# Projection blocks of the forgetting-attention heads taken in pairs, seven pairs with 2x2 block products; weight sums formed by transfers in memory

## Chip, core and metric

One core of one Trainium2 chip runs one layer of a hybrid decoder trunk. The metric is the device time of one execution in microseconds. The engines are PE (TensorE, its weight loads shown apart as PEld), DVE (VectorE), ACT (ScalarE), POOL (GpSimd) and SP (SyncE, which here only issues transfers).

## What is computed

A layer of width 2048 over 16 meta tokens and 512 tokens. A normalised input goes through one input projection, whose columns feed three kinds of heads: six gated DeltaNet heads, five gated linear attention heads (GLA) and five forgetting-attention heads. Each head's output is multiplied by a SiLU gate, and all go through one output projection, a residual add and a final norm.

```python
def hybrid_layer(x, norm_w, w_in, ...):
    h = rms_norm(x, norm_w)
    h = jnp.pad(h, ((0, 0), (PAD, 0), (0, 0)))
    proj = (h @ w_in).astype(f32)
    (dq, dk, dv, dz, db, da, gq, gk, gv, gz, gl, fq, fk, fv, fz, ff) = split_cols(proj)
    ...
    o_dn = gated_head_norm(o_dn, dz, dn_norm_w.astype(f32))
    ...
    o_gla = gated_head_norm(o_gla, gz, gla_norm_w.astype(f32))
    ...
    o_fox = forgetting_attention(to_heads(fq, FOX_HEADS) * FOX_D ** -0.5, to_heads(fk, FOX_HEADS),
                                 to_heads(fv, FOX_HEADS), log_f)
    o_fox = o_fox.reshape(fz.shape) * jax.nn.silu(fz)
    o = jnp.concatenate([o_dn, o_gla, o_fox], axis=-1)[:, PAD:].astype(x.dtype)
    return x + o @ w_out
```

Everything is float32, to float32 accuracy.

## The kernel before

**Numbers.** A float32 operand of a large product is split into two parts of a shorter type: `hi`, a rounded copy written by ACT, and `lo`, the rest, written by DVE (`split`, lines 148 to 151). A product is then three: hi x hi, hi x lo, lo x hi.

**Input projection.** The transposed input lies on chip for the whole projection as 16 row blocks of 128 features (`xh[k]`, `xl[k]`, each 128 x 528: 16 meta tokens and 512 tokens). The weights are in blocks of 128 output columns, each in two halves of 8 row blocks (`w_in[b, half]`, 128 x 1024, 512 KB). `load_half` (line 140) issues a half's load on SP's queue into `raw`, and splits it into `hi` and `lo`; each of these three has two buffers. `inproj` (221) runs a block. With the meta tokens it makes two results of 264 columns, so 16 x 3 x 2 = 96 products; without them (`meta=False`: fq, fz, gates) one result of 512 columns with 48 products. Results go to banks of the pool `psb`, which has four; `evac` (320) multiplies them by the row factor `rstd` of the norm on their way out.

**Order.** The blocks run in the order of `_cols`: for each of two groups of three DeltaNet heads dz, then dk (`dn_keys`), dv (`dn_values`), dq (`dn_queries`); then gz, the GLA blocks by pairs of heads (`gla_pair`), then for each forgetting head fk, fv, fq, fz (`fox_head`). The small work of a stage (scores, state products, transposes) runs between the products of later blocks. A planner orders all instructions of each engine when the kernel is built, by program order as priority and by its own estimates of time. On the chip each engine takes its instructions in that fixed order. `behind` and `place` tie some small products behind a numbered product of the projection; in particular `behind(mm, PM[g])` ties the first product `pm` of a group's triangular inverse behind the 308th (group 0) or 319th (group 1) product after `dn_queries`.

**The triangular inverse** (`dn_inverse`, line 535). Blocks of the matrix `an` go through memory (`scr`) into `ab`, DVE inverts them by 60 dependent steps (lines 556 and 558), the result goes through memory (`sc2`) into `iv`, and the products `pm`, `pl`, `pn`, `pu` put the pieces together. These transfers are on ACT's queue.

**SiLU** (`silu`, line 330) begins with a maximum on POOL (line 334), has three steps on ACT and one product on DVE.

**Output projection.** Heads 0 to 7 of the list dz, gz, fz (the six DeltaNet gates and two GLA gates; `SH = 8`) go through it as 2x2 blocks by seven products (`product`, 1151); the other eight as plain products (`run`, 1094). The seven products need sums of weight blocks, `tw`. `weight_sums` (426) forms them in the stage of forgetting heads 0 to 3: it loads 256 KB parts into `ws`, subtracts on DVE (432) and stores them to `tw`. `first_sums` (452) forms the sums of the heads on DVE in forgetting head 4. The gated heads stay on chip in the pool `zp` until then.

## Time and profile before

| | |
|---|---|
| three runs | 1011.84, 1010.10, 1010.04 us; median 1010.1 |
| profiled execution | 1010.53 us |
| its span, first to last instruction | 1008.8 us |
| granted TensorE clock, mean | 0.998 |
| bytes moved by transfers | 128.13 MB, 127 GB/s over the span |
| input projection, forgetting-attention stage | 631 to 828 us |
| GLA stage | 486 to 631 us |
| output projection | 828 to 1001 us |

The profiler gives each instruction's start and duration. A group of rows shows line, engine, operation, out<-in by the program's names, shape, count, then busy time in us, the mean duration of one in ns, the idle time of the engine just before these, and what ended that idle time. Products overlap: the spacing of their starts is what a product costs in a stream, not its duration. Of transfers the rows give count, size of one in KB and the median time from issue to landing in us.

### The profile page before, as it was taken

The page shows a single profiled execution, that of the slowest core. Times are in us where ns is not written, and L with a number is a line of the kernel's source. Part 1 is how long each engine was busy: PE and PEld are TensorE (multiplying, and loading weights), DVE is VectorE, ACT ScalarE, POOL GpSimd, SP SyncE. Part 2 cuts the span into 40 slices and gives each one's busy share as a digit, 9 for nine tenths or more (in the row PEclk, how much of TensorE's full clock was granted, in tenths as well). Part 3 has the DMA queues.
Part 4 walks back from the last instruction along what each step waited for, and adds up shares of the span by engine and source line. Part 5 has one row for each costly group of instructions (what it writes and reads, how often), then busy time and mean ns, then how long its engine had stood idle before and what let it go on. Part 6 is the DMA issues. An engine that isn't in the chain of part 4 may idle for free.

```text
span 1008.8 us, 19003 instructions
## 1 busy us (share of the span) xinstructions
PE 995.7 (99%) x7614; PEld 898.7 (89%) x7614; DVE 618.2 (61%) x1342; ACT 433.1 (43%) x948; POOL 138.6 (14%) x141
## 2 busy tenths in 40 slices
PE   9999999999999999999999999999999999999996
PEld 7899999899999888898989988889898988888885
DVE  6366767865566985244646474655363747677673
ACT  7654533434456334244445444342323244354354
POOL 0021411211112322101111010100101010000060
PEclk9999999999999999999999999999999999999999
DMA  9623233233222223231221272543362635466634
GB/s 351 229 67 119 82 93 96 102 101 104 75 86 75 94 90 101 68 94 59 84 64 50 66 244 82 189 138 93 120 226 95 237 119 188 127 193 226 181 109 167
DMA packets 53357, 128.13 MB, mean 127 GB/s; under 512 B 11949, under 2 KB 15197, under 8 KB 53268
## 3 DMA queue, kind: packets, MB, share of 16 engines
q1 hardware_dynamic: 39008, 115.30, 34.5%
q10 hardware_dynamic: 14260, 11.61, 4.1%
q8 instruction: 60, 0.98, 0.4%
q14 instruction: 29, 0.24, 0.1%
HBM read 113.32 MB, written 13.44 MB: 126 GB/s over the span
## 4 chain that ended last, share of the span: by engine, by line
PE 92%; DVE 3%; ACT 1%; DMA 1%; POOL 1%; issue 1%; ACTq 1%; SPq 0%; DVEq 0%; POOLq 0%
PE pp L207 57%; PE pa L1068 5%; PE pq L1068 4%; PE pp L261 4%; PE pt L1068 4%; PE ps L1068 2%; PE pss L822 1%; PE pr L1068 1%; POOL stgz L334 1%; PE pgate L361 1%; PE pfo L990 1%; PE pfa L957 1%; DVE wlo L151 1%; DVE ot L556 1%; PE pg L523 1%
## 5 line engine op out<-in xcount | busy, mean ns | idle before, releaser
L207 PE MATMUL pp<-xl,whi 128*128 128x264 f32 (+2 forms) x1456 | 378.1, 310 | 0.0
L207 PE MATMUL pp<-xh,whi 128*128 128x264 f32 (+2 forms) x1456 | 376.3, 310 | 0.8 <-DVE fqk L325 0.7
L207 PE MATMUL pp<-xh,wlo 128*128 128x264 f32 (+2 forms) x1456 | 375.4, 309 | 0.4 <-DVE wlo L151 0.4
L207 PEld LDWEIGHTS pp<-xh,whi 128*128 128x128 f32 x1456 | 243.1, 188 | 15.1 <-issue 1.4
L207 PEld LDWEIGHTS pp<-xl,whi 128*128 128x128 f32 x1456 | 244.3, 189 | 13.6 <-issue 0.2
L207 PEld LDWEIGHTS pp<-xh,wlo 128*128 128x128 f32 x1456 | 243.7, 188 | 14.1 <-DVE wlo L151 0.8
L150 ACT CAST whi<-raw 128x1024 fp32r<-128x1024 f32 x110 | 115.3, 1048 | 184.7 <-PE pp L207 158.1
L151 DVE TENSOR_TENSOR wlo<-raw,whi 128x1024 fp32r<-128x1024 f32 x110 | 134.4, 1222 | 88.8 <-ACT whi L150 78.2
L334 POOL TENSOR_SCALAR stc<-cv 128x528 f32<-128x528 f32 (+1 forms) x18 | 28.2, 1566 | 138.2 <-DVE cv L418 115.2
L418 DVE SCALAR_TENSOR_TENSOR cv<-pb,cpk,cv 128x528 f32<-128x528 f32 (+1 forms) x54 | 40.7, 755 | 0.7
L1068 PE MATMUL pa<-whio,ol 128*128 128x512 f32 x72 | 28.5, 396 | 0.0
L1068 PE MATMUL pa<-wloo,oh 128*128 128x512 f32 x72 | 28.3, 393 | 0.0
L325 DVE TENSOR_TENSOR pb<-pp,rstd 128x264 f32<-128x264 f32 (+1 forms) x36 | 13.7, 423 | 23.3 <-PE pp L207 23.3
L432 DVE TENSOR_TENSOR ws<-ws 128x512 f32<-128x512 f32 x32 | 21.6, 686 | 9.7 <-DMA ws<-in_w_dn 9.6
L150 ACT CAST whis<-raws 128x1024 fp32r<-128x1024 f32 x16 | 16.8, 1051 | 24.8 <-PE pq L1068 9.7
L151 DVE TENSOR_TENSOR wlos<-raws,whis 128x1024 fp32r<-128x1024 f32 x16 | 19.5, 1222 | 12.7 <-ACT whis L150 12.7
L1068 PE MATMUL pa<-whio,oh 128*128 128x512 f32 x72 | 26.6, 399 | 0.0
L977 ACT CAST fphi<-pfx 128x384 fp32r<-128x384 f32 (+2 forms) x20 | 8.0, 399 | 41.0 <-PE pfx L974 38.2
L966 ACT ACTIVATE fp<-fp,fsm 128x144 f32<-128x144 f32 (+3 forms) x20 | 11.5, 574 | 29.8 <-DVE fsm L965 29.7
L150 ACT CAST whio<-rawo 128x1024 fp32r<-128x1024 f32 x13 | 13.7, 1051 | 24.1 <-PE pa L1068 12.8
L334 POOL TENSOR_SCALAR stfz<-zfz 128x512 f32<-128x512 f32 x5 | 10.6, 2126 | 94.9 <-ACT whi L150 47.8
L1092 POOL TENSOR_TENSOR acc<-acc,fw 128x512 f32<-128x512 f32 x3 | 4.6, 1564 | 135.2 <-ACT sqf L1089 135.2
(439 smaller groups left out, 1642.7 us busy)
## 6 DMA issues: line engine op xcount, KB each, us to landing
raw<-in_w_in SPq DMA_DIRECT2D x110, 512.0 KB, 3.3
ws<-in_w_dn SPq DMA_DIRECT2D x32, 256.0 KB, 4.7
tw<-ws SPq DMA_DIRECT2D x32, 256.0 KB, 3.5
rawo<-in_w_out SPq DMA_DIRECT2D x13, 512.0 KB, 3.4
raws<-tw SPq DMA_DIRECT2D x12, 512.0 KB, 4.6
xt<-in_xtok SPq DMA_DIRECT2D x8, 512.0 KB, 8.7
rawa<-in_w_dn SPq DMA_DIRECT2D x8, 512.0 KB, 3.6
xs<-in_xT SPq DMA_DIRECT2D x7, 528.0 KB, 7.1
```

The source lines that it names most:

```text
L150: pace[0] = A.copy(hi, raw).ins
L151: pace[1] = V.tensor_tensor(out=lo, in0=raw, in1=hi.bitcast(F32), op=ALU.subtract).ins
L207: mm = PE.matmul(p_[:, :nt], wt[:, j * m : (j + 1) * m], xx[k][:, t0 : t0 + nt], start=(k == 0 and wt is hi and xx is xh), stop=(k == KT - ...
L261: mm = PE.matmul(ps[:, :S], wt[:, j * P : (j + 1) * P], xx[k][:, NM:T], start=(k == 0 and wt is hi and xx is xh), stop=(k == KT - 1 and wt ...
L325: V.tensor_tensor(out=o, in0=p_[rows], in1=rstd[rows, t0 : t0 + n], op=ALU.mult)
L334: G.tensor_scalar_max(t, src, LOW)
L361: PE.matmul(pgate[a][:, :HT], wg[k // 8][:, k % 8, :], xx[k][:, a * HT : (a + 1) * HT], start=(k == 0 and xx is xh), stop=(k == KT - 1 and ...
L418: V.scalar_tensor_tensor(out=c, in0=pb[:, t0 + w : w + T], scalar=cwc[:, blk, w : w + 1], in1=c, op0=ALU.mult, op1=ALU.add)
L432: sub = lambda o, a, b: V.tensor_tensor(out=o, in0=a, in1=b, op=ALU.subtract)
L523: PE.matmul(pg[:r, j * r : (j + 1) * r], kT[:, j, ts], kT[:, j, ts], start=True, stop=True)
L966: A.activation(pr[:, : m + P], pr[:, : m + P], AF.Exp, bias=sm[:, 2:3], accum_out=sm[:, 3:4])
L1068: PE.matmul(p_, o_[:, s], w_, start=(first and n == 0), stop=(last and n == 2), skip_group_check=True)
```

## The change

It has three parts.

**Pairs of projection blocks.** For forgetting heads 1 to 4 the blocks are taken as pairs (fk, fq) and (fv, fz). The first pair of head 1 runs as before (`SKIP = 1`), which leaves seven. `inproj_pair` treats a pair as a 2x2 block product: output blocks (one, two) by token halves of 264 columns, over row blocks k and k + 8. For 4 of the 8 pairs of row blocks (`NK = 4`) it uses seven products with sums of weights and of inputs; the other four pairs of row blocks are plain. Its weights come as six tiles, split in halves of 512 columns; some are negated in the split. The columns of the meta tokens of the second block are left out where they are not needed (`dead`). The results are scaled by `rstd` afterwards, on POOL and DVE.

```diff
+    def inproj_pair(n, c1, c2, tmp):
...
+            for c in range(0, o, 512):
+                cuts.append(slice(c, c + 512))
+                split(raw[:, cuts[-1]], hi[:, cuts[-1]], lo[:, cuts[-1]], neg)
+            return [(hi[:, c], lo[:, c]) for c in cuts]
+
+        def mm(p_, w, xx, first=False, last=False, cols=slice(0, HT)):
+
+            hi, lo = w
+            todo = [(hi, j, i) for j in range(len(xx)) for i in range(2)] + [(lo, j, 0) for j in range(len(xx))]
+            for i, (wt, j, part_) in enumerate(todo):
+                m = PE.matmul(p_[:, cols], wt[:, j * P : (j + 1) * P], xx[j][part_][:, cols],
+                              start=first and i == 0, stop=last and i == len(todo) - 1, skip_group_check=True)
+                order.append(m.ins)
...
+        dead = slice(NM, HT)
+        nm = f"{b1}_"
+        a, b = bank("a"), bank("b")
+        w1, w2 = tile_of("1", both(b1, head_))
+        mm(a, w1, xs_(up, lo_), True, True)
+        A.copy(ta, a[:, :HT])
+        mm(b, w2, xs_(dn, lo_), True)
+        def two():
+            nonlocal d
+            d = bank("d")
+            w1, w2 = tile_of("2", ti[n][:, 0:2], neg=True)
+            mm(d, w1, sums("t1"), True, True)
+            A.copy(tb, d[:, :HT])
+            mm(a, w2, sums("t2"), False, True)
+            V.tensor_tensor(out=tb, in0=a[:, :HT], in1=tb, op=ALU.add)
+
+        def three():
+            nonlocal c
+            c = bank("c")
+            w1, w2 = tile_of("3", both(b1, rest_))
+            mm(b, w1, xs_(r0, lo_))
+            mm(b, w2, xs_(r1, lo_), False, True)
+            V.tensor_tensor(out=c1[:, lo_], in0=b[:, :HT], in1=ta, op=ALU.add)
+            mm(c, w1, xs_(r0, hi_), True)
+            mm(c, w2, xs_(r1, hi_))
+
+        c = d = None
+        for f in (three, two) if n < LATE else (two, three):
+            f()
+        w1, w2 = tile_of("4", ti[n][:, 2:4])
+        mm(a, w1, xs_(up, hi_), False, True)
+        A.copy(ta, a[:, :HT])
+        mm(c, w2, xs_(dn, hi_), False, True)
+        V.tensor_tensor(out=c1[:, hi_], in0=c[:, :HT], in1=tb, op=ALU.add)
+        w1, w2 = tile_of("5", w_in[b2, 0][:, rest_], w_in[b2, 1][:, head_], neg=True)
+        mm(d, w1, xs_(r0, hi_))
+        mm(a, w2, sums("t4"), cols=dead)
+        mm(a, w1, xs_(r0, lo_), cols=dead)
+        w1, = tile_of("6", w_in[b2, 1][:, rest_], neg=True)
+        mm(d, w1, xs_(r1, hi_), False, True)
+        V.scalar_tensor_tensor(out=c2[:, hi_], in0=d[:, :HT], scalar=-1.0, in1=ta, op0=ALU.mult, op1=ALU.subtract)
+        mm(a, w1, xs_(r1, lo_), False, True, cols=dead)
+        A.activation(c2[:, dead], a[:, dead], AF.Copy, scale=-1.0)
```

In `fox_head` the seven pairs and their scaling:

```diff
+                inproj_pair(n, kT, qT, qk[:, 1])
+                G.tensor_tensor(out=kT, in0=kT, in1=rstd, op=ALU.mult)
+                V.scalar_tensor_tensor(out=qT[:, NM:], in0=qT[:, NM:], scalar=float(P) ** -0.5, in1=rstd[:, NM:],
+                                       op0=ALU.mult, op1=ALU.mult)
+            if h == H1:
+                x_last(True)
+            v = row(f"vf{h}")[:, :T]
+            zr = row(f"zfz{h}")[:, :T]
+            inproj_pair(n + 1, v, zr, qk[:, 1])
+            G.tensor_tensor(out=v, in0=v, in1=rstd, op=ALU.mult)
+            vhi, vlo, v3, vm = values(v)
+            G.tensor_tensor(out=zr[:, NM:], in0=zr[:, NM:], in1=rstd[:, NM:], op=ALU.mult)
```

**Input sums.** `x_sums(k)` forms three sums of input blocks for row block k with nine operations on POOL, and splits each (ACT and DVE). It stands before GLA pair 1 for k = 0, before pair 2 for k = 1 and 2, and in forgetting head 0 for k = 3. `x_last` replaces the second token half of `xh[0..3]` and `xl[0..3]` by a sum, formed in head 0 on DVE and written in head 1 before its pair. The sums of k = 0 to 2 take buffers of `zp` (12 instead of 11). To free those, the eight heads of the 2x2 output blocks are stored to memory (`zd`) when they are done, and loaded again after the last projection block.

**Weight sums in memory.** `weight_sums` goes. For the pairs (`ti`) and for the output projection (`tw`), sums are formed by a copy from memory to memory on SP's queue and transfers that add to their destination, on POOL's queue. Signs are chosen so that all are additions. Each `load_half` issues up to `rate` = 2 such steps, from `dn_values(0)` on, tied behind the split of that load in the planned order (`paced`, an order only, not a wait). A group of jobs goes stage by stage: all copies, then the additions that read only weights, then the two that read earlier results.

```diff
+    def steps_of(jobs):
+        for kind, out_, in_ in jobs:
+            if kind:
+                paced(G.dma_start(out=out_, in_=in_, accum_op=ALU.add, max_dma_last_dim=2048))
+            else:
+                paced(nc.sync.dma_start(out=out_, in_=in_))
+            yield 1
+
+    def in_jobs(n):
+        h, one, two = PAIRS[n]
+        w = lambda key, half: w_in[BLOCK_OF[key, h], half][:, :KC]
+        o = [ti[n][:, i] for i in range(4)]
+        return [[(0, o[0], w(two, 0)), (0, o[2], w(one, 0)), (0, o[1], w(one, 0)), (0, o[3], w(one, 1))],
+                [(1, o[0], w(two, 1)), (1, o[2], w(two, 0))], [(1, o[1], o[0])], [(1, o[3], o[1])]]
+
+    def out_jobs(j):
+        w = lambda i, J: w_dn[J, 2 * j + i]
+        o = [tw[j, i] for i in range(4)]
+        return [[(0, o[0], w(0, 1)), (0, o[2], w(1, 1)), (0, o[1], w(1, 1)), (0, o[3], w(1, 0))],
+                [(1, o[0], w(0, 0)), (1, o[2], w(0, 1))], [(1, o[1], o[0])], [(1, o[3], o[1])]]
...
+    AHEAD = {(0,0):(2,(-1,-2,-3,-4),(-5,-6,-7),(0,1,2,3))}
+    XSUM = {1: (0,), 2: (1,2), 9:(3,)}
```

`KC` is 512 columns, so a step of a pair moves 256 KB and one of the output projection 512 KB. The order is four pairs, three pairs, then the four output blocks.

With other signs, the output projection subtracts instead of adding where it takes up the second half of its columns (`take`), and `first_sums`, `differences` and `s4` follow. `first_sums` moves to POOL and to the third step of the output projection. In `fox_head` the buffer of the next head's keys and queries is taken early (`ahead_`), and in `gla_pair` the tile `a32` shares the buffer of `ot`.

241 lines of the change are left out of this document (177 added, 64 removed).

## The prediction

> **What bounds the kernel now.** I read the page's sums first, then the chain that ended last, then stage windows, then who waits for whom.
>
> ```profile
> span 1008.8 us, 19003 instructions
> PE 995.7 (99%) x7614; PEld 898.7 (89%) x7614; DVE 618.2 (61%) x1342; ACT 433.1 (43%) x948; POOL 138.6 (14%) x141
> PE 92%; DVE 3%; ACT 1%; DMA 1%; POOL 1%; issue 1%; ACTq 1%; SPq 0%; DVEq 0%; POOLq 0%
> ```
>
> TensorE is busy for 995.7 of 1008.8 us and is 92% of the chain. Busy alone doesn't prove that it streams, so I looked at starts. Two stretches of the projection, one of products 264 columns wide (a row merges two), one 512 wide, and three products 256 wide:
>
> ```profile
> 731.12 0.41 PE L207 MATMUL pp<-xh,whi 128*128 128x264 f32 x2
> ...
> 738.98 0.41 PE L207 MATMUL pp<-xh,wlo 128*128 128x264 f32 x2
> 700.42 0.39 PE L207 MATMUL pp<-xh,wlo 128*128 128x512 f32 x1
> ...
> 708.07 0.39 PE L207 MATMUL pp<-xh,wlo 128*128 128x512 f32 x1
> 715.15 0.28 PE L990 MATMUL pfo<-fphi,vhi 128*128 128x256 f32 x1
> 715.26 0.28 PE L990 MATMUL pfo<-fplo,vhi 128*128 128x256 f32 x1
> 715.38 0.29 PE L990 MATMUL pfo<-fphi,vlo 128*128 128x256 f32 x1
> ```
>
> The first stretch holds 64 products between its quoted starts (32 rows of two): 7.86 / 64 = 0.1228 us each. The second holds 33: 7.65 / 33 = 0.2318. The third shows 0.115. The slope between the first two is (0.2318 - 0.1228) / 248 = 0.00044 us a column, so a 248-wide product should take 0.1228 - 16 x 0.00044 = 0.1158. These are spacings; the 0.41 or 0.39 in a row is a duration that overlaps its neighbours.
>
> TensorE's waits on anything else are small:
>
> ```profile
> PE pp L207 <- DVE fqk L325: 0.7, 1, 0.7
> PE psn L694 <- ACT y L690: 0.6, 1, 0.6
> PE pp L207 <- DVE wlo L151: 0.4, 1, 0.4
> 631.00:828.00 197.00, 196.31 (x1232) 176.34 (x1232) 105.54 (x261) 65.46 (x128) 15.17 (x16) 1.00 0.46 154
> ```
>
> The window is the forgetting-attention stage, 631 to 828 us (columns: length, then busy time of PE, weight load, DVE, ACT, POOL, then granted clock, DMA share, GB/s). TensorE is full there at a granted clock of 1.00; DVE is at 54%, ACT at 33%, POOL at 8%. So what counts is TensorE work removed, less new waits of TensorE; work moved between the other engines counts only through such waits.
>
> **The products.** Before, a pair such as fk and fq costs 96 products of 264 and 48 of 512: 96 x 0.1228 + 48 x 0.2318 = 11.79 + 11.13 = 22.92 us. After, I count the calls of `mm` in `inproj_pair`: fifteen, each of 4 x 3 products, so 180. Three calls (36 products) write only columns 16 to 263, the others 264: 144 x 0.1228 + 36 x 0.1158 = 17.68 + 4.17 = 21.85. A pair saves 1.07 us, seven save 7.5. If the 248-wide ones took a full 0.1228, it would be 0.82 a pair, 5.7 in all; at the 0.115 of the 256-wide row, 1.10 and 7.7.
>
> The Trainium skill's page "TensorE: Matmul & The Clock Gate", section "Back-to-back issue gap", speaks against such a trade: for streams of weight load and product it gives some 81 ns at 128 columns and 131 at 512, so width would cost little and count much. As an estimate from that page, 264 columns would be about 99 ns; a pair would go from 15.8 to 17.8 us and the seven would lose 14. The rows disagree, with 0.1228 against 0.2318.
>
> **The weight tiles of a pair.** Six tiles feed a pair instead of four, in halves of 512 columns; four of them feed only 24 products, 24 x 0.1228 = 2.95 us, where before each fed 5.6 to 5.9.
>
> ```profile
> raw<-in_w_in SPq DMA_DIRECT2D x110, 512.0 KB, 3.3
> L150 ACT CAST whi<-raw 128x1024 fp32r<-128x1024 f32 x110 | 115.3, 1048 | 184.7 <-PE pp L207 158.1 <-issue 10.0 <-DVE vpm L633 8.7
> L151 DVE TENSOR_TENSOR wlo<-raw,whi 128x1024 fp32r<-128x1024 f32 x110 | 134.4, 1222 | 88.8 <-ACT whi L150 78.2 <-PE ps L653 4.3 <-ACT gsq L897 4.2
> SPq L142 <- DVE wlo L151: 524.2, 86, 13.2
> ws<-in_w_dn SPq DMA_DIRECT2D x32, 256.0 KB, 4.7
> ```
>
> Today SP waits for a free raw buffer and ACT for TensorE to give a buffer back (158.1 of 184.7 us idle), so supply has room. One buffer's round is 3.3 + 1.05 + 1.22 = 5.6 us, two buffers give a tile every 2.8: just under 2.95, well under the pair's mean of 21.85 / 6 = 3.6. With a load of 4.7 us (the slowest weight row) it is (4.7 + 2.27) / 2 = 3.5, late by 0.54 us at each of three short tiles in a row (6, 1, 2): 1.6 a pair, 11.3 in all. I take 0.1 a pair, 0.7, since the mean has room and half tiles let the first product start after 512 columns; bounds 0 and 11.3.
>
> **The banks.** A product that accumulates onto a bank must wait until the copy out of it is done. For six pairs 24 to 48 products stand between. Pair 0 runs block three ahead of two, so tile 4's products onto bank a stand right behind the DVE sum that reads a. That is the kind of wait in the row "PE pp L207 <- DVE fqk": 0.7 us, once. Bounds 0 and 0.7 for each pair, 4.9.
>
> **Work off TensorE.** ACT and DVE split 38.5 full tiles where they split 28 (seven pairs by 5.5 and 4): 10.5 x 1.22 = 12.8 us more on DVE, and four reads of a bank a pair. DVE loses the weight sums (32 x 0.686) and the work moved to POOL.
>
> ```profile
> L432 DVE TENSOR_TENSOR ws<-ws 128x512 f32<-128x512 f32 x32 | 21.6, 686 | 9.7 <-DMA ws<-in_w_dn 9.6
> L1092 POOL TENSOR_TENSOR accs<-accs,fw 128x512 f32<-128x512 f32 x9 | 13.3, 1511 | 0.0
> 486.00:631.00 145.00, 142.96 (x1894) 130.79 (x1893) 88.74 (x190) 65.89 (x173) 16.49 (x12) 1.00 0.31 99
> ```
>
> POOL's nine operations of 264 columns for each of four row blocks (`x_sums`), scaled from 1.511 us for 512, are 9 x 0.78 = 7 us a block. Three blocks fall into 486 to 631 us, where POOL is busy 16.5 of 145. POOL's scaling of kT and v (1.6 us each) and DVE's of qT are hidden by the next pair's 21.85 us or by the head's scores. I cost all this, `x_last`, the eight gates stored and read back, and `first_sums` on POOL (needed some 30 us later) at nothing. Without cover, a late kT costs its 1.6 us in each of four heads.
>
> **The traffic in memory.** 88 steps go out at two a weight load over 44 loads, from dv of the first group to the last gz. They move 28 copies of 256 KB and 16 of 512, and as many accumulations, and end some 240 us before the first pair needs them. Each is issued behind a split, copies on SP, accumulations on POOL. Behind a copy on SP stand the weight loads, which have room as shown. Behind an accumulation on POOL stand silu's first step and the masks; POOL idles 86% of the time, but one place has no room: the triangular inverse of group 1. The chain of waits:
>
> ```profile
> 341.27 1.79 DMA scr<-an
> 354.85 3.50 POOL stgz L334
> 366.48 2.65 POOL stgz L334
> 377.65 2.61 POOL stgz L334
> 386.61 5.46 DMA sc<-ab
> 395.14 0.58 DVE L568 STREAM_TRANSPOSE iv<-iv 128x384 f32<-128x384 f32 x1 [5.62 <-DMA iv<-sc]
> 396.57 0.95 PE L574 MATMUL pm<-iv,an 32*32 32x32 f32 x48
> 214.22 0.58 DVE L568 STREAM_TRANSPOSE iv<-iv 128x384 f32<-128x384 f32 x1 [3.14 <-DMA iv<-sc]
> 220.48 0.95 PE L574 MATMUL pm<-iv,an 32*32 32x32 f32 x48
> ```
>
> The inverse is a serial run on DVE, and three silus of gz stand in its queue, each held by POOL (stgz). Its result is ready at 395.72 and TensorE takes it at 396.57: 0.85 us of room, where group 0 has 220.48 - 214.80 = 5.7. TensorE takes its work in order, so what comes later than 0.85 us is paid in full. The last 16 accumulations, of 512 KB, go out over the eight loads of gz1 to gz4, right there.
>
> No row shows what an accumulation costs POOL. Nearest are ACT's own issues (0.33 us at L541, in the row below) and stgz itself at 2.61:
>
> ```profile
> 338.42 0.33 ACTq L541
> 338.78 1.93 ACTq L541
> ```
>
> Three silus, each behind one issue, give 1.0 to 7.8 us, and transfers scr, sc and iv (1.79, 5.46 and the end of sc at 392.07 to 395.14 = 3.07; sum 10.3) may stretch by nothing up to double. Less the 0.85: 0.1 to 17 us. I take 1.5: half the silus behind an issue of some 1.0 us (the mean of the two ACT issues is 1.1) and a tenth of the transfers, 1.5 + 1.0 - 0.85 = 1.6; it lies near the low end because POOL is idle before each stgz and the accumulations stop before sc goes out.
>
> The page "DMA: Bandwidth & Descriptors" of the Trainium skill, section "Anatomy of one DMA — SWDGE (gpsimd) path", gives a DMA from GpSimd some 2.0 us plus its bytes over 436 GB/s. By it a 512 KB accumulation is an estimated 3.2 us and 16 of them 51 us in a stretch of some 45; the transfers would be slowed to the end of the chain. No row of before can show it.
>
> **The sum**, against the profiled execution's 1010.53 us (span 1008.8, 1.7 around it; 0.4 above the median 1010.1 of 1010.04 to 1011.84): -7.5 products, +0.7 tiles, +0.7 bank, +1.6 inverse = -4.5. From the median: 1005.6.
>
> **Rivals.** (1) *No new wait*: the chain keeps inside its 0.85 us and the tiles are in time: 1010.1 - 7.5 = 1002.6. For it: POOL and DMA are mostly idle (a DMA share of 0.31 and 0.46 in the windows). Against: the chain's small room.
> (2) *Short tiles starve*: loads of 4.2 us make a tile cost 3.24 instead of 2.95, three a pair, 21 x 0.29 = 6.1 in place of 0.7: 1005.6 + 5.4 = 1011.0, no change. For it: the 2.8 us round; against: SP's long waits.
> (3) *The inverse is late, slower than before*: scr, sc and iv double under the copies and accumulations (+10.3), silus add 1.5: 11.8 - 0.85 = 11.0 in place of 1.6: 1015.0. It decides from a delay of 1.6 + 4.5 + 2 + 0.85 = 9.0 us on. For it: it all passes at 341 to 395 us; against: the traffic is spread over loads.
> (4) *Weight loads show*: 36 more per pair that nothing hides at 0.188 us (its row below) are 6.8 a pair, 47 in all: 1053. Loads start every 0.12 us today beside products, so hardly. The Trainium skill's rule on the gap, above, leads the same way.
> (5) *Sums not ready*: tile 2 waits for memory. The last accumulation is due before 400 us, the first pair runs near 690; 290 us of room leave it next to nothing.
>
> ```profile
> L207 PEld LDWEIGHTS pp<-xl,whi 128*128 128x128 f32 x1456 | 244.3, 189 | 13.6 <-issue 0.2
> ```
>
> **How the numbers follow.** Forecast 0.50, (1) 0.20, (2) 0.13, (3) 0.15, (4) and (5) together 0.02. About 0.2%, 2 us, is what a measurement tells from no change. Faster: 0.50 + 0.20 = 0.70; same 0.13; slower 0.17. The forecast's own range is 1003.6 (inverse and tiles free, bank paid) to 1008. For 8 in 10 I reach down to 1001.8 (rival 1 with 7.7 and ordering) and up to 1011.8 (all of rival 2); left out is most of (3).
>
> **What would show it.** Right: in a stretch of pairs 264-wide starts 0.123 apart and 248-wide 0.115 to 0.117; seven pairs' products 153 us in all against 160; a wait of TensorE near pm of group 1 of 1 to 2 us; bank waits below 1 us. Wrong: waits of TensorE on wlo or whi in the pairs above 2 us in sum (rival 2), a wait at pm above 5 us or stgz starting late behind POOL's issues (rival 3), or 264-wide starts further apart than 0.125.

## The result, and the profile after

| | before | after |
|---|---|---|
| median of six runs each, same chip | 1010.06 us (1009.27 to 1011.84) | 1014.4 us (1013.65 to 1016.73) |
| ratio | | 1.0046, 95% interval 1.0036 to 1.0057 |
| profiled execution | 1010.53 us | 1014.15 us |
| granted TensorE clock, mean | 0.998 | 0.995 |
| bytes moved | 128.13 MB | 152.57 MB |

The kernel became slower by 0.46%, where 0.45% faster was forecast; 1014.4 lies outside the range of 1001.8 to 1011.8. The sums on the page of the changed kernel, and its chain that ended last:

```profile
span 1012.4 us, 19797 instructions
PE 991.5 (98%) x7866; PEld 908.5 (90%) x7866; DVE 642.7 (63%) x1389; ACT 460.4 (45%) x1041; POOL 224.5 (22%) x236
PE 49%; DVE 2%; issue 1%; DMA 1%; ACT 1%; ACTq 0%; SPq 0%; DVEq 0%
```

TensorE is busy for 4.2 us less than before in a span that is 3.6 us longer. The chain's shares add up to little more than half, so it breaks off on the way back and can't be read as before. The view of TensorE's waits can (total, times, longest, in us):

```profile
PE pm L735 <- DVE iv L729: 2.7, 1, 2.7
PE py L849 <- DVE zz L845: 1.9, 1, 1.9
PE pp_b L533 <- DVE wlo L167: 1.1, 1, 1.1
PE pp_a L533 <- ACT fqk L575: 1.0, 1, 1.0
```

Two of these four were in the sum (pp_b is the wait for a tile, pp_a the wait for a bank, both in the first pair). The one at pm was there with a smaller size, and the one at py not at all.

**Where the time went.** For six groups of TensorE's products, the start of the last one, as the rows grouped by tile give it, in us (for "first pa", the start of the first of L1295's products with `wloo`). The two right-hand columns are experiments told below.

| | before | after | output sums left out (e6) | output sums first, begun earlier (e11) |
|---|---|---|---|---|
| pu, end of the inverse of group 1 | 421.6 | 425.6 | 422.1 | 423.9 |
| po, end of the DeltaNet stage | 480.7 | 488.0 | 481.7 | 483.5 |
| pgt, end of the GLA stage | 631.7 | 641.1 | 634.2 | 634.3 |
| first pa, start of the output projection | 828.8 | 830.2 | 823.4 | 823.4 |
| last pz | 1000.4 | 1004.1 | 995.6 | 995.6 |

Read as lags behind the kernel before: +4.0 at pu, +7.3 at po, +9.4 at pgt, +1.4 at the output projection, +3.7 at the end. So the stage with the pairs did gain 8.0 us, its own new waits included, but it began 9.4 us late; 7.3 of that arose in the DeltaNet stage, which the change was not about. The next two groups of windows, first of the kernel before, then of the changed one (length, busy time of PE, weight load, DVE, ACT, POOL, then granted clock, DMA share, GB/s), show that place:

```profile
396.00:410.00 14.00, 13.62 (x204) 11.16 (x203) 5.57 (x9) 6.48 (x11) 0.00 (x0) 1.00 0.21 76
410.00:486.00 76.00, 75.42 (x590) 70.97 (x589) 27.63 (x67) 29.55 (x97) 8.08 (x7) 1.00 0.24 74
```

```profile
396.00:410.00 14.00, 11.29 (x169) 9.68 (x169) 4.17 (x7) 6.84 (x11) 0.42 (x2) 0.88 0.61 184
410.00:486.00 76.00, 73.49 (x600) 69.11 (x588) 28.82 (x68) 27.78 (x87) 16.96 (x17) 0.98 0.55 147
401.42:404.83 3.41, 3.41 (x15) 3.19 (x14) 0.37 (x2) 2.37 (x4) 0.00 (x0) 0.50 0.86 298
466.27:469.68 3.41, 3.41 (x18) 3.41 (x18) 2.14 (x6) 0.00 (x0) 0.00 (x0) 0.50 0.70 127
```

TensorE stands still for 2.7 us of the first window. The DMA share is 0.61 and 0.55 where it was 0.21 and 0.24. And the granted clock, 1.00 throughout before, is at one half for 3.41 us twice: the drops begin 1.7 and 2.0 us after the two waits have ended, and each costs up to 3.41 x 0.5 = 1.7 us of products.

**The wait at pm.** The timeline of the changed kernel along the inverse of group 1 (start, duration, engine; in brackets the idle time before and what ended it):

```profile
386.46 0.26 ACTq L721 DMA_DIRECT2D sc<-ab  x1
...
394.66 0.38 ACTq L724 DMA_DIRECT2D iv<-sc  x1
...
398.47 0.69 DVE L354 TENSOR_TENSOR zsgz<-zgz,stgz 128x512 f32<-128x512 f32 x1 [9.05 <-ACT stgz L353]
399.08 0.57 DVE L729 STREAM_TRANSPOSE iv<-iv 128x384 f32<-128x384 f32 x1
399.70 0.95 PE L735 MATMUL pm<-iv,an 32*32 32x32 f32 x48 [2.71 <-DVE iv L729]
```

The store sc is issued at 386.46, before at 386.61: DVE's inverse and the silus in its queue were on time. From the issue of sc to that of iv it now takes 8.20 us (before 5.48), from there to the transpose 4.42 (before 3.05). Together that is 4.1 us more, against 0.85 us of room. The two parts have different causes.

The first 2.7 us are the store sc, and it is held up ahead of its first packet. The view of transfers of the changed kernel between 386.5 and 391.4 us shows packets of one queue alone, SP's (packets, MB, share of the 16 engines):

```profile
q1 hardware_dynamic: 176, 1.46, 85.0%
```

On that queue a weight load and two copies of 512 KB had been issued at 384.8, 385.2 and 385.7 us. By the packet records of the trace, the first packet of sc starts 4.97 us after its issue and the last ends 2.71 us after that; in the kernel before it is 1.27 and 3.85 us. So sc is not slower while it moves.

The other 1.4 us are not the transfer iv: its packets, with those of `xm` behind it, end 2.9 us after its issue, and before 3.0. They are the order of DVE's queue. Here `zsgz`, the last step of a silu, stands ahead of the transpose of iv, and it waits for ACT's silu steps, which stand behind the issues of iv and `xm` in ACT's queue. In the kernel before it stands behind the transpose of 395.14:

```profile
396.30 0.69 DVE L338 TENSOR_TENSOR zsgz<-zgz,stgz 128x512 f32<-128x512 f32 x1
```

The planner made this order when the kernel was built. Of the runs below, e3, e4 and e8, which have two output copies just ahead of sc as well, have it too, and all others have the order of before.

**The wait at py.** The timeline of the changed kernel, then that of the one before, for the fetch `eg`, the decay factors of a chunk of the DeltaNet recurrence:

```profile
448.16 2.75 POOL L436 DMA_DIRECT2D tw<-in_w_dn  x3
...
456.46 0.37 ACTq L834 DMA_DIRECT2D eg<-gd  x1
462.02 0.52 ACT L835 ACTIVATE eg<-eg 128x384 f32<-128x384 f32 x1 [4.69 <-DMA eg<-gd]
...
462.58 0.17 DVE L837 COPY egl<-eg 128x3 f32<-128x3 f32 x1 [6.40 <-ACT eg L835]
...
464.29 1.01 PE L849 MATMUL py<-zz,uf 128*128 128x128 f32 x6 [1.94 <-DVE zz L845]
```

```profile
452.52 0.37 ACTq L673 DMA_DIRECT2D eg<-gd  x1
456.08 0.53 ACT L674 ACTIVATE eg<-eg 128x384 f32<-128x384 f32 x1 [2.68 <-DMA eg<-gd]
```

The fetch takes 5.56 us instead of 3.56. DVE takes its instructions in order, so `zz`, which does not need `eg`, stands behind the copy `egl` that does, and TensorE behind `zz`.

**What ran beside them.** Rows of the changed kernel by tile (shortest, median and longest issue in ns, first and last start in us) and its transfers (KB of one, median us from issue to landing):

```profile
L438 SPq DMA_DIRECT2D tw<-in_w_dn x16: 488/498/606, 367.7 to 432.3; - x16
L436 POOL DMA_DIRECT2D tw<-in_w_dn x8: 894/1216/1925, 448.2 to 478.2; - x8
L436 POOL DMA_DIRECT2D tw<-tw x8: 891/1260/1881, 481.0 to 536.0; - x8
tw<-in_w_dn SPq DMA_DIRECT2D x16, 512.0 KB, 5.7
tw<-in_w_dn POOLq DMA_DIRECT2D x8, 512.0 KB, 8.6
```

The sixteen copies of the output sums stand around sc, the first accumulations beside eg. The fetch eg too is held up ahead of its first packet, by the packet records: 3.58 us from its issue (before 1.24), and then 1.62 us of moving (before 1.99). All of this traffic was forecast to be over before sc went out. `load_half` takes its two steps with `next(chores[0], None) or chores.pop(0)`: a list that has run out uses up a chance without issuing a transfer. There are 11 groups of jobs in 4 lists each, so 88 steps use 88 + 44 = 132 chances, 66 loads and not 44.

### The profile page after: what moved, and what is told of

Same layout as the page of the kernel before. It is cut to its first block, busy times and chain, and to the rows that moved or that the text cites. A ratio compares the mean times of both kernels' runs of the same rounds, so it can differ in the third digit from the quotient of the medians.

```text
span 1012.4 us, 19797 instructions
## 1 busy us (share of the span) xinstructions
PE 991.5 (98%) x7866; PEld 908.5 (90%) x7866; DVE 642.7 (63%) x1389; ACT 460.4 (45%) x1041; POOL 224.5 (22%) x236
## 2 busy tenths in 40 slices
DMA packets 64194, 152.57 MB, mean 151 GB/s; under 512 B 12925, under 2 KB 16173, under 8 KB 63844
## 4 chain that ended last, share of the span: by engine, by line
PE 49%; DVE 2%; issue 1%; DMA 1%; ACT 1%; ACTq 0%; SPq 0%; DVEq 0%
PE pp L223 13%; PE pp_a L533 6%; PE pa L1295 5%; PE pt L1295 4%; PE pq L1295 3%; PE pp_d L533 3%; PE pp_c L533 3%; PE pp_b L533 3%; PE ps L1295 1%; PE pss L983 1%; PE pr L1295 1%; PE pfo L1186 1%; DMA raws<-in_w_dn 1%; PE pfa L1153 1%; PE pfx L1170 1%
## 5 line engine op out<-in xcount | busy, mean ns | idle before, releaser
L223 PE MATMUL pp<-xl,whi 128*128 128x264 f32 (+2 forms) x1120 | 285.2, 307 | 0.0
L223 PE MATMUL pp<-xh,wlo 128*128 128x264 f32 (+2 forms) x1120 | 283.1, 306 | 1.5 <-issue 1.5
L223 PE MATMUL pp<-xh,whi 128*128 128x264 f32 (+2 forms) x1120 | 283.2, 306 | 0.8 <-DVE fqk L341 0.8
L223 PEld LDWEIGHTS pp<-xh,wlo 128*128 128x128 f32 x1120 | 187.3, 189 | 10.5 <-issue 2.1
L223 PEld LDWEIGHTS pp<-xh,whi 128*128 128x128 f32 x1120 | 187.0, 189 | 10.3 <-DVE fqk L341 1.0
L223 PEld LDWEIGHTS pp<-xl,whi 128*128 128x128 f32 x1120 | 187.7, 189 | 9.0 <-issue 0.2
L167 DVE TENSOR_TENSOR wlo<-raw,whi 128x1024 fp32r<-128x1024 f32 (+1 forms) x124 | 129.4, 1054 | 89.9 <-ACT whi L166 83.9
L166 ACT CAST whi<-raw 128x1024 fp32r<-128x1024 f32 (+1 forms) x124 | 109.8, 902 | 165.4 <-PE pp L223 120.6
L162 ACT ACTIVATE whi<-raw 128x512 fp32r<-128x512 f32 x35 | 20.5, 624 | 25.0 <-PE pp_c L533 10.3
L166 ACT CAST whis<-raws 128x1024 fp32r<-128x1024 f32 x16 | 16.4, 1048 | 29.1 <-DMA raws<-tw 10.3
L1295 PE MATMUL pa<-whio,ol 128*128 128x512 f32 x72 | 28.4, 395 | 0.0
L1295 PE MATMUL pa<-wloo,oh 128*128 128x512 f32 x72 | 28.4, 395 | 0.0
L533 PE MATMUL pp_a<-xh,whi 128*128 128x264 f32 (+1 forms) x112 | 27.9, 283 | 0.0
L533 PE MATMUL pp_a<-xl,whi 128*128 128x264 f32 (+1 forms) x112 | 27.7, 281 | 0.0
L1295 PE MATMUL pa<-whio,oh 128*128 128x512 f32 x72 | 25.9, 400 | 0.0
```

Of the source, the lines that this page charges most:

```text
L162: pace[0] = A.activation(hi, raw, AF.Copy, scale=-1.0).ins
L166: pace[0] = A.copy(hi, raw).ins
L167: pace[1] = V.tensor_tensor(out=lo, in0=raw, in1=hi.bitcast(F32), op=ALU.subtract).ins
L223: mm = PE.matmul(p_[:, :nt], wt[:, j * m : (j + 1) * m], xx[k][:, t0 : t0 + nt], start=(k == 0 and wt is hi and xx is xh), stop=(k == KT - ...
L533: m = PE.matmul(p_[:, cols], wt[:, j * P : (j + 1) * P], xx[j][part_][:, cols], start=first and i == 0, stop=last and i == len(todo) - 1, ...
L1295: PE.matmul(p_, o_[:, s], w_, start=(first and n == 0), stop=(last and n == 2), skip_group_check=True)
```

## The experiments

Theory T: the loss is the output sums' transfers beside sc, iv and eg, with the clock's drop behind each wait. Rivals: the pairs' transfers or loads cost something too; the work on ACT, DVE and POOL does; or the place on the chain is at fault, not the traffic. Ratios are to the kernel before in the same comparison, with 95% intervals.

### e1: no sums in memory at all

```diff
-    AHEAD = {(0,0):(2,(-1,-2,-3,-4),(-5,-6,-7),(0,1,2,3))}
+    AHEAD = {}
-            w1, w2 = tile_of("2", ti[n][:, 0:2], neg=True)
+            w1, w2 = tile_of("2", both(b1, head_), neg=True)
-    product(pa, "s2", lambda j: tw[j, 1], False, True)
+    product(pa, "s2", lambda j: w_dn[1 % 2, 2 * j], False, True)
...
```

> The changed kernel without the weight sums in memory: no copies, no accumulations; tiles 2 and 4 of the pairs and the output products that need sums load plain weights of the same size instead, so the number of products, splits and loads is the same and the values are not. Theory T (the loss comes from the traffic, which stretches the transfers sc, iv and eg that group 1 of DeltaNet waits for): the waits of TensorE at pm (2.7 us) and at py (1.9 us) go, and the two drops of the granted clock after them; time 1014.4 - 2.7 - 1.9 - 2.2 = about 1007, and lower if the output stage's 2.3 us go too. Rival P (the loss comes from the pairs' own side work: input sums on POOL, gates stored and read back, a changed plan): the two waits stay at 2 us or more each and the time stays above 1012.

Measured: 1004.7 us against 1009.4, ratio 0.9954 (0.9939 to 0.9969). The view of TensorE's waits:

```profile
PE py L848 <- DVE zz L844: 0.6, 1, 0.6
```

The wait at pm is gone, the one at py is 0.6 us, and the clock stays up. The loss comes with the traffic, the changed order of DVE's queue included, since here DVE has the order of before. Everything else in the change is worth -4.7 us, a little more than theory T expected.

### e6: the pairs' sums alone; e8: and the output copies, without their accumulations

e6 leaves the four output groups out of the list and loads plain weights in the place of their sums, e8 leaves out only their last three stages:

```diff
-    AHEAD = {(0,0):(2,(-1,-2,-3,-4),(-5,-6,-7),(0,1,2,3))}
+    AHEAD = {(0,0):(2,(-1,-2,-3,-4),(-5,-6,-7))}
```

```diff
-                [(1, o[0], w(0, 0)), (1, o[2], w(0, 1))], [(1, o[1], o[0])], [(1, o[3], o[1])]]
+                [], [], []]
```

> As the changed kernel, but no sums for the output projection are formed at all; its products load plain weights of the same size, so their values are not the reference's. It prices the pairs' own 56 transfers against the run without any traffic (1004.7). Theory T, sharpened: no difference, 1004 to 1006, so the output sums' 32 transfers carry all of the loss. If traffic costs by its bytes: half of the 9.7 us, about 1009.

> The changed kernel without the 16 accumulations of the output sums; their 16 copies stay at their places (367 to 432 us), so the values of the output are not the reference's. Theory T: the copies stretch sc and iv, the accumulations from 448 us on stretch eg. So the wait at pm stays at 2 to 3 us with its clock drop, the wait at py goes: time about 1009 to 1011. If accumulations alone are to blame, both waits go: about 1005.

Measured: e6 1005.47 us, ratio 0.995 (0.9935 to 0.9965); e8 1009.77, ratio 0.9994 (0.9983 to 1.0004). Of e6 and e8 the rows of the store sc, of the fetch iv and of pm in the timelines:

```profile
387.37 0.26 ACTq L721 DMA_DIRECT2D sc<-ab  x1
392.87 0.38 ACTq L724 DMA_DIRECT2D iv<-sc  x1
...
397.74 0.95 PE L735 MATMUL pm<-iv,an 32*32 32x32 f32 x48
```

```profile
386.26 0.26 ACTq L721 DMA_DIRECT2D sc<-ab  x1
396.02 0.38 ACTq L724 DMA_DIRECT2D iv<-sc  x1
...
400.43 1.28 PE L735 MATMUL pm<-iv,an 32*32 32x32 f32 x48 [3.63 <-DVE iv L729]
```

e6 equals e1 within the intervals of 0.15%, so in their place the pairs' 56 transfers cost less than can be measured. They are not without effect: beside two of their copies the second eg of group 0 takes 6.5 us (before 3.7), and TensorE waits 0.96 us at 272 us. With the output copies sc takes 9.76 us instead of 5.50 (its first packet starts 5.28 us after its issue), TensorE waits 3.6 us at pm, and a drop of the clock follows at 400.78; with no accumulations eg takes 3.3 us and the wait at py is gone. So the copies make the wait at pm and the accumulations the one at py: by the ratios about 0.44% or 4.4 us from e6 to e8, and 0.52% or 5.3 us from e8 to the changed kernel, the latter from two comparisons. Both times came out as theory T expected.

### e4: the kernel before, with the traffic added

The steps and their `AHEAD` order go into the kernel before, into buffers that nothing reads; its own weight sums on DVE stay.

```diff
+        for _ in range(rate[0]):
+            if chores:
+                next(chores[0], None) or chores.pop(0)
...
+        if g == 0:
+            rate[0] = 2
+            for js in ((-1, -2, -3, -4), (-5, -6, -7), (0, 1, 2, 3)):
+                jobs(*[in_jobs(-k - 1) if k < 0 else out_jobs(k) for k in js])
```

> The kernel before, with the same 88 copies and accumulations issued at the same loads (its own weight sums stay as they were; the new sums are not used). Theory T: the traffic alone makes waits at pm and py of group 1 and drops of the clock, 4 to 7 us: 1014 to 1017. Rival P: the time stays within 2 us of 1010.

Measured: 1021.0 us against 1009.4, ratio 1.0111 (1.0096 to 1.0126), more than expected. TensorE's waits:

```profile
PE py L725 <- DVE zz L721: 3.1, 2, 2.4
PE pm L611 <- DVE iv L605: 2.8, 1, 2.8
```

The same two waits appear where nothing else was changed, and here too `zsgz` stands ahead of the transpose of iv. The span, 1019.6 us, is 10.8 us longer than before; the waits are 5.9, and the clock is at half for 6.83 us from 400.75 and 3.41 us from 469.0, which is up to 5.1 more. The expectation had drops of the clock in it, but counted 4 to 7 us for waits and drops together.

### e3: the inverse's products tied 26 products later

```diff
-    PM = (308, 319)
+    PM = (308, 345)
```

> The changed kernel with group 1's inverse products tied behind the 345th product instead of the 319th, so 26 x 0.122 = 3.2 us later in TensorE's order; the traffic stays as it is. If only the small room at pm was short: the wait at pm (2.7 us) and the clock drop behind it (about 1 us net) go, the wait at py stays; time about 1011. If the chain behind pm (pl, pn, the mix) is short of room as well, the wait moves on to it and the time stays at 1013 to 1015.

Measured: 1011.16 us (1008.55 to 1016.91, the widest spread of all), ratio 1.0019 (1.0002 to 1.0035). Its waits:

```profile
PE pp L223 <- ACT whi L166: 2.6, 1, 2.6
```

The wait at pm is gone and has come back at 399 us as a wait for a weight tile, with one drop of the clock at 403.9. Rows of its timeline:

```profile
397.56 0.38 ACTq L724 DMA_DIRECT2D iv<-sc  x1
...
400.61 1.03 ACT L166 CAST whi<-raw 128x1024 fp32r<-128x1024 f32 x1
```

ACT issues iv only when sc has landed, here 11.0 us after the issue of sc (the last packet of sc ends at 397.2), and the silu steps and the split of the next weights stand behind that issue in ACT's queue. So a late sc reaches TensorE through ACT's queue as well as through iv, with a wait of about the same length. The wait at py, expected to stay, is gone (0.9 us in two parts): the third eg goes out later, at 462.3, and takes 3.2 us. That part of the gain on the changed kernel is luck of timing.

### Other places for the output sums: e2, e7, e5, e9

e2 makes each chance count and begins the output sums in the third GLA pair. e7 makes each chance count and takes one step a load from dk of group 0 on.

```diff
-                next(chores[0], None) or chores.pop(0)
+            step()
+    def step():
+        while chores and not next(chores[0], None):
+            chores.pop(0)
-    AHEAD = {(0,0):(2,(-1,-2,-3,-4),(-5,-6,-7),(0,1,2,3))}
+    AHEAD = {(0,0):(2,(-1,-2,-3,-4),(-5,-6,-7)), ("g",2):((0,1,2,3),)}      # e2
+    AHEAD = {(0,-1):(1,(-1,-2,-3,-4),(-5,-6,-7),(0,1,2,3))}                 # e7
```

e5 and e9 form the output sums on DVE, as the kernel before does, with additions: e5 in forgetting heads 0 to 3, e9 behind the first two GLA pairs.

```diff
+    def weight_sums(j, half):
...
+        get(x, 0, 1)
+        get(y, 0, 0)
+        get(z, 1, 1)
+        sub(y, x, y)
+        sub(x, z, x)
+        sub(z, z, y)
...
+        if h in SUMS:                                       # e5, in fox_head
+            for j, half in SUMS[h]:
+                weight_sums(j, half)
+        for j in ((0, 1), (2, 3), ())[p]:                   # e9, behind gla_pair(p)
+            for half in range(2):
+                weight_sums(j, half)
```

> The 32 steps for the output projection start with GLA pair 2 instead of right behind the pairs' steps, and a step is issued at every chance (an exhausted list no longer uses up one). So no copy or accumulation runs from about 310 to 560 us. Theory T: sc takes 5.5 us again instead of 8.2, iv 3.0 instead of 4.4, the waits at pm and py fall below 1 us each, the clock stays at 1.00; time about 1007 to 1008. Rival P: the waits stay, time 1013 to 1015. A third reading, that traffic costs the same wherever it lies: the waits appear in the GLA or attention stage instead, time 1012 to 1015.

> All 88 steps kept, one a load instead of two, starting with the dk blocks of group 0; no chance goes unused. The traffic is the same but thinner: it runs from about 80 us to the end of attention head 1. If the density next to the waited-for transfers decides: the waits at pm and py drop to about 1 us each, the clock stays up, time about 1008 to 1010. If any traffic beside such a transfer costs alike: 1013 to 1016, with smaller waits at more places.

> The changed kernel with the sums for the output projection formed as in the kernel before (loaded, added on DVE, stored, in attention heads 0 to 3), the pairs' sums still formed in memory. Theory T, sharpened: only the output sums' traffic (367 to 550 us) meets transfers that TensorE waits for, the pairs' part (88 to 365 us) meets none. Then the waits at pm and py fall to 0.9 us or less, the clock stays at 1.00 and the time is 1004 to 1006, faster than the kernel before. If the 512 KB loads and stores of these sums crowd the pairs' six weight tiles in the attention stage, waits on wlo of 2 to 5 us there and 1007 to 1010. Rival P: 1013 or more.

> The output projection's sums formed by loads, additions on DVE and stores as before, but behind GLA pairs 0 and 1, where each weight tile feeds 5.6 us or more of products, instead of in the attention stage, where four of the six tiles feed 2.95 us. The pairs' sums stay in memory. Theory T with the finding of the run with these sums in the attention stage (short tiles leave no room for other loads): waits at pm and py below 1 us, GLA stage no more than 3 us longer than before's, attention stage as in the changed kernel; time 1005 to 1008, faster than before. If the 32 loads and 32 stores crowd GLA as they crowd the pairs: 1012 or more.

| | time, us | ratio |
|---|---|---|
| e2 | 1022.3 | 1.0142 (1.0114 to 1.0171) |
| e7 | 1021.15 | 1.012 (1.0103 to 1.0137) |
| e5 | 1023.26 | 1.0126 (1.0111 to 1.0141) |
| e9 | 1046.61 | 1.0379 (1.0363 to 1.0394) |

All four are slower than the changed kernel and than their expectations, but for the "1012 or more" of e9. The largest wait of TensorE in each, of e2, e7, e5 and e9 in turn:

```profile
PE pss L986 <- issue: 4.7, 3, 2.3
```

```profile
PE pp_b L536 <- ACT whi L169: 3.7, 1, 3.7
```

```profile
PE pp_d L533 <- ACT whi L162: 4.4, 4, 2.8
```

```profile
PE pss L1003 <- DVE kq L989: 26.7, 4, 10.1
```

In e2 the wait at pm is gone, but no chance is lost, so the pairs' steps stand closer together (their last copy goes out at 223.5 us instead of 285.2), and TensorE waits beside or just behind them: 1.65 us until 175 and 1.07 until 223 for weight tiles, and 1.90 until 279 at py, where the second eg takes 8.3 us. More waits and three drops of the clock come beside and behind the output sums, from 566 us on. In e5 the DeltaNet stage is clean (its window 396 to 410 has 14.00 us of PE), but the attention stage takes 19 us longer than in the changed kernel, with waits for short tiles of the pairs (`whi L162`) and for work on DVE; that the loads and additions beside them are the cause is argued, not separated. In e7 the wait at pm is gone and py is down to 0.95 us, as the reading by density had it, but one step a load makes the last eight accumulations go out between 624 and 830 us, and its wait of 3.7 us is at 809, among them. In e9 the additions stand in DVE's queue ahead of the GLA steps `kq` that TensorE waits for:

```profile
501.11 1.29 DVE L611 TENSOR_TENSOR ws<-ws 128x512 f32<-128x512 f32 x2
502.31 0.42 DVE L985 TENSOR_TENSOR kq<-gqk,gdd 128x256 f32<-128x256 f32 x1
```

### Order and start: e10, e11, e12

e10 takes the output sums first, from the same load on; e11 does that from dk of group 0 on, six loads earlier; e12 keeps the order and only starts earlier.

```diff
-    AHEAD = {(0,0):(2,(-1,-2,-3,-4),(-5,-6,-7),(0,1,2,3))}
+    AHEAD = {(0,0):(2,(0,1,2,3),(-1,-2,-3,-4),(-5,-6,-7))}      # e10
+    AHEAD = {(0,-1):(2,(0,1,2,3),(-1,-2,-3,-4),(-5,-6,-7))}     # e11
+    AHEAD = {(0,-1):(2,(-1,-2,-3,-4),(-5,-6,-7),(0,1,2,3))}     # e12
```

> The changed kernel with the three groups of steps in another order: the output sums' 512 KB steps first, then the pairs' 256 KB steps. Bytes and number of steps are the same. If it is the place that decides: group 0's inverse, with 5.7 us of room, now meets the large copies and shows nothing or up to 1 us; group 1's meets half the bytes a step, so its waits at pm and py are 1 to 2 us in sum and the granted clock drops at most once; time 1008 to 1011. If total bytes decide: 1014 as the changed kernel.

> As the run with the output sums first, but starting six loads earlier, with the dk blocks of group 0, so that all steps end some 35 us earlier, near 515 us. If only steps beside group 1's transfers cost: the same or up to 2 us less than the run with the later start; if the transfers of group 0's keys and inverse suffer: a wait at pm of group 0 (near 221 us) and 1 to 4 us more.

> The sums in the order of the changed kernel (the seven pairs first, the output weights last), but begun six weight loads earlier, at dk of group 0, as the fastest version so far does (1006.8, output weights first). It tells whether that version gains by its order or by its start. In the changed kernel the output copies went out at 367 to 432 us and their accumulations at 448 to 536; six loads earlier that is some 45 to 70 us earlier: copies at about 305 to 380, accumulations at about 390 to 480. Theory S (what costs is a 512 KB transfer beside sc, iv or eg, whatever the order): sc then stands clear of the copies, but iv (392 to 396) and eg (about 456) stand beside accumulations, so eg stays above 4.5 us and TensorE's wait at py stays near 2 us with a drop of the clock; the wait at pm falls from 2.7 to 0.5 to 2 us. Time 1009 to 1013. Rival O (the start alone is enough): both waits fall below 0.7 us, no drop, 1005.5 to 1007.5, as with the other order.

| | time, us | ratio | clock at half |
|---|---|---|---|
| e10 | 1015.92 | 1.0066 (1.0050 to 1.0082) | 6.83 us at 223.0, 3.41 at 407.3 |
| e11 | 1006.82 | 0.9972 (0.9962 to 0.9982) | none |
| e12 | 1008.61 | 0.9985 (0.9974 to 0.9996) | 3.41 us at 400.9 and at 520.4 |

The largest waits of TensorE in e10, then in e11 (at 218 and 402 us), then in e12:

```profile
PE py L849 <- DVE zz L845: 3.0, 3, 1.6
PE pp L223 <- DVE wlo L167: 2.5, 2, 1.9
PE pm L735 <- DVE iv L729: 2.2, 1, 2.2
```

```profile
PE pp L223 <- DVE wlo L167: 1.8, 2, 1.3
```

```profile
PE pm L735 <- DVE iv L729: 2.4, 1, 2.4
```

In e10 the 512 KB accumulations (148 to 231 us) stand beside the inverse of group 0, which was thought safe with 5.7 us of room: there sc goes out 3.3 us later than before and takes 7.4 us instead of 4.9, and TensorE waits for a tile at 220 us, with the long drop behind it. In group 1 only the pairs' 256 KB transfers are left, and they were expected to cost 1 to 2 us there: the waits are 2.2 us at pm, where iv takes 5.3 us beside three of their accumulations, and 1.6 at py. So the place counts for more than which sums the traffic is for. e11 has issued the last 512 KB step by 190 us and is the only version with all the sums whose profile has no drop. It is faster than both kernels, and 9 us faster than e10 where at most 2 were expected. It is not free of the effect: sc of group 1 still takes 7.0 us beside the pairs' copies, but TensorE comes to pm 1.8 us late, since its wait at 218 us, and so finds iv ready. In e12 the last copies (330 to 388 us) run into sc, which takes 7.1 us, and the wait at pm stays; the wait at py is gone, against the expectation, though accumulations of 512 KB go out at 448 to 479: eg took 3.6 us. Only two of them are issued just before it, at 448.4 and 449.0, where the changed kernel has three, at 448.2, 448.8 and 449.4, and while eg is under way the packet records show 50 KB on POOL's queue in e12 and 510 KB in the changed kernel. So they were nearly over. The time lies between the two that were expected. Starting six loads earlier is worth 0.6% (1.0046 to 0.9985); whether the order adds to that is not settled, the intervals of e11 and e12 overlap.

## Why the prediction was wrong

**The products: right.** Rows of the changed kernel's timeline within a pair:

```profile
660.58 1.14 PE L533 MATMUL pp_d<-t,whi 128*128 128x264 f32 x8
...
663.52 0.29 PE L533 MATMUL pp_c<-xh,whi 128*128 128x264 f32 x1
...
674.13 0.28 PE L533 MATMUL pp_a<-xh,whi 128*128 128x248 f32 x1
...
676.41 0.62 PE L533 MATMUL pp_a<-xh,wlo 128*128 128x248 f32 x4
```

24 products stand between the first two starts (x8, x4, x8, x4): 2.94 / 24 = 0.1225 us, forecast 0.1228. 20 stand between the last two: 2.28 / 20 = 0.114, forecast 0.1158. A pair is then 144 x 0.1225 + 36 x 0.114 = 21.74 us instead of 21.85, and seven save 8.3 instead of 7.5. Rival 4, weight loads that show, is ruled out by the same spacings, and with it the rule of the Trainium skill's page "TensorE: Matmul & The Clock Gate", section "Back-to-back issue gap", by which 264 columns would have been an estimated 99 ns.

**Tiles and banks: the sizes about right, by luck.** The waits are 1.1 and 1.0 us for 0.7 and 0.7, each once, in the first pair, but neither is where the prediction had it. The wait for a tile is at tile 3, which feeds 48 products and is not short: DVE works without a pause from 644.6 to 656.4 us, and the additions of `x_last` (`xe`, `xl`), costed at nothing, stand between the splits. The wait for a bank is not at tile 4 behind DVE's sum but at tile 5, behind ACT's copy out of bank a (L575), which itself waits for DVE. Rival 2 did not happen: in the changed kernel, e1 and e6 the six other pairs show no wait for a tile of 0.2 us or more. Waits for short tiles do come where large transfers lie beside the pairs (e5, e7). Rival 5 is ruled out: the sums are in memory by about 545 us, the first pair begins at 650 (near 690 in the prediction, which has both 240 and 290 us for this room).

**The traffic in memory: the step that failed.** The prediction put the inverse at 1.6 us, with "a tenth of the transfers" (1.0 us), since "the accumulations stop before sc goes out"; any other transfer beside the traffic, and the clock, were not in its sum. Four things in it were wrong.
- When: 88 steps were spread over 44 loads, which is how many would do if each chance issued a step. A third of the chances are lost, so the largest transfers came last, over the inverse of group 1 and the recurrence behind it.
- How much: from the issue of sc to the transpose it took 4.1 us longer, not 1.0: 2.7 us because sc waited behind the copies on SP's queue, and 1.4 because DVE's queue had another order. The 1.5 us that were put on silu behind POOL's issues did not occur: POOL's step of the last of these silus starts at 388.2 us, before at 387.8.
- Who else: only the transfers of the inverse were counted. The fetch eg is on ACT's queue too, and DVE's queue has no room behind it: 1.9 us.
- What follows: a wait was costed at its length. The clock's drop behind it adds up to 1.7 us.

With what was measured, against the profiled 1010.53 us: products -8.3, tile and bank +2.1, pm 2.7 and py 1.9, two drops up to 3.4: +1.8. The profiled execution shows +3.6, and stage by stage the differences are larger. By the lags, the DeltaNet stage lost 7.3 us (the terms give up to 8.0), GLA 2.1 and the output projection 2.3 (no term), and the stage with the pairs gained 8.0 (the terms give 6.2).
- In GLA, TensorE's waits that the profile marks `issue` are 2.3 us against 1.5 before, and 0.8 us of waiting for `fqk` has moved there from the stage with the pairs (0.7 before). Without its waits at `issue` the stage takes 150.8 to 150.9 us in the changed kernel, e6 and e11; e11 has none of them, which is why its GLA stage is shorter.
- The output projection takes 173.9 us from its first pa to its last pz, against 171.6 before. In e6, e8, e10, e11 and e12, which have the same products there, it takes 172.2. The other 1.7 us are this execution's: loads of `raws` land late, and at 939 to 949 us TensorE waits three times for their tiles. Why they land late, and whether the other executions have it, is open.

Without the output sums the forecast's terms would have been -7.5 + 0.7 + 0.7 = -6.1, or 1004.0; e6 is at 0.995 of 1010.1, 1005.0. So the rest of the sum was right to about 1 us. Its own lower bound, 1003.6, comes out at 1003.3 by its terms (1005.6 - 1.6 - 0.7), which changes nothing.

**The rivals.** Rival 3 had the right mechanism, transfers of the inverse slowed by the copies and accumulations, and a total close to the truth (1015.0) for a partly wrong reason: it doubled all three transfers, 10.3 us, where scr was not late, sc grew by half (2.7 of 5.5 us) and iv not at all; what filled it up to 1014.4 was the order of DVE's queue, eg and the clock, which it lacked. That the totals agree is luck. Against it the prediction held that "the traffic is spread over loads"; the count of chances in the code would have shown that this spread puts the largest copies where the room was 0.85 us.

**What stays open.** Why the packets of sc and eg start so late behind those of another queue: the records show that they do, not by what rule. Why the planner put `zsgz` ahead of the transpose wherever the output copies stand there; no run has both copies with the order of before, so the 1.4 us, and whether the drop behind pm would come without them, are not tested alone. (e12 has one copy just ahead of sc and the order of before: sc takes 7.1 us, and TensorE still waits 2.4 us at pm, but there sc also goes out 2.4 us later.) What the waits at `issue` in the GLA stage are.

## What to carry to other kernels

Traffic that nobody waits for is not free: before giving it a place, list every small transfer whose result TensorE waits for within a few us, on all queues, and keep large transfers away from those, from just ahead of their issue on, not only from the stage that needs the result. See whether the engines' queues kept their order, since the planner may change it when instructions are added. Count the issues of a paced list from the code as it runs, exhausted entries included, since the last ones land latest. And cost a wait of TensorE of about 2 us or more at its length plus a clock drop behind it.

## What the runs showed of the hardware that was not expected

**The clock falls after waits of about 2 us.** Over all the profiles between 20 and 980 us (e9 aside), each of the eight waits of TensorE of 2.38 us or more saw a drop begin between 0.8 us before its end and 2.3 us after it. Of the eleven waits of 1.9 to 2.3 us six did: the one of 1.94 us at 462.4 in the changed kernel did, the one of 2.29 us at 565.8 in e2 did not. Two waits of 1.66 and 1.51 us with 1.4 us between them were followed by one as well in e7 (668.7) and e2 (679.9); two of 1.63 and 1.51 us with the same spacing in e5 (673.8) were not. In these runs a drop is to one half, for 3.41 or 6.83 us. The Trainium skill's page "TensorE: Matmul & The Clock Gate" tells of a free-running window of 3413 ns ("What's actually happening") and asks for no idle gaps over some 3 us ("Why this matters for your kernels"). The lengths of the drops agree with that window; the gaps don't agree with the advice, 1.94 us was enough here, though not each time.

**Large copies on one queue held up a small transfer on another ahead of its first packet, the more the more bytes they had.** The time from the issue of sc in group 1 to its first packet, by the copies that SP issued in the 1.3 us before, behind a weight load:

| copies just ahead of sc | run | us to the first packet |
|---|---|---|
| none | before, e6 | 1.27, 1.21 |
| two of 256 KB | e11 | 2.40 |
| one of 512 KB | e12 | 2.48 |
| two of 512 KB | changed kernel, e3, e4, e8 | 4.97, 4.99, 4.33, 5.28 |

The moving itself takes 3.85 us before and 2.71, 4.40, 4.07 and 3.98 in the runs of the last line. The third eg of group 1 starts after 3.58 us instead of 1.24 and then moves in 1.62 instead of 1.99. Moving can be slower too: the second eg of group 0 takes 3.66 us for it in e6, beside the pairs' copies, against 1.47 before. So 256 KB transfers do it as well; the pairs' own were cheap in the changed kernel because TensorE had room there, and where it had none they cost up to 2.2 us at one wait (e2, e10).

**An accumulating transfer takes longer than a copy of its size**: 8.6 us against 5.7 for 512 KB, and 0.9 to 1.9 us of POOL for each issue. The two are on different queues, and the accumulations go out up to three in a row, so waiting for each other is in their median. By the page "DMA: Bandwidth & Descriptors" of the Trainium skill it was an estimated 3.2 us in the prediction; the row says 2.7 times that.
